# Layer 0's projection of a two-layer diffusion transformer: a fixed TensorE order, modulation in column tiles, x in half rows

## The chip, the core and the metric

The kernel runs on one core of a Trainium2 chip. Its engines work beside each other, each through its own list of instructions in order: TensorE (PE in the rows, with its weight loads as PEld), VectorE (DVE), ScalarE (ACT), GpSimd (POOL) and SyncE (SP), which here starts nearly all DMA transfers. The metric is the device time of one launch in microseconds (us), median of several runs. Lower is better.

## The reference, cut to what matters

The program computes two layers over 1024 latent tokens and 256 context tokens, 1024 features each, in float32. The change lies in the first step of layer 0: the modulation vectors, the modulated input h, and its product with the input weights.

```python
for l in range(DEPTH):
    m_lat = [m[:, None, :] for m in jnp.split(jax.nn.silu(c) @ ada_w[l] + ada_b[l], 6, axis=-1)]
    m_ctx = jnp.split(jax.nn.silu(c_ctx) @ ada_w[l] + ada_b[l], 6, axis=-1)
    h_lat = modulate(x_lat, m_lat[0], m_lat[1])      # x * (1 + scale) + shift
    h_ctx = modulate(x_ctx, m_ctx[0], m_ctx[1])
    ...
# layer 0: even_mixer -> even_project
qa, ka, va, qb, kb, vb = jnp.split(h @ w_in, [...], axis=-1)
return (rms_norm(heads(qa, A_HEADS), q_gain), rms_norm(heads(ka, A_KV_HEADS), k_gain),
        heads(va, A_KV_HEADS), heads(qb, B_HEADS), heads(kb, B_HEADS), heads(vb, B_HEADS))
```

Two kinds of attention, an output product and a convolutional feed-forward layer follow, and then layer 1. The change leaves them as they are.

## The kernel before, in words

Tokens go in ten tiles of 128: tiles 0 to 7 are latent (H[0] holds 0 to 3, H[1] 4 to 7), 8 and 9 are context (H[2]). Every operand of a product is split into a high and a low part, so one product is three matmuls for each of the eight feature blocks k (`mm3`, lines 333 to 337): 24 matmuls.

The stage `l0_project` runs in this order. `ada_first` (line 141) makes the first two modulation vectors (shift and scale) of layer 0 for the latent and the context condition: 16 loads `wt` of 512 KB, each used by two matmuls that give 2 rows x 512 columns (line 160); the sums get their bias (line 170) and are transposed in 16 pieces (line 173). Then x and the context are loaded in 10 tiles of 512 KB (lines 445 and 447), each feature block of each group is transposed (line 452), scaled and shifted by ScalarE (`sg`, line 456), and split into `hh` (line 462) and `hl` (line 464, by turns on VectorE and GpSimd). Then come five blocks of weights: columns 512 (k and v of attention A, 256 wide), 0 (its q), 1792 (v of attention B) by `proj_tok`, 768 and 1280 (q and k of attention B) by `proj_feat`. Each is loaded by `load_in` through the pool `raw`, which has two buffers of 512 KB, and split by `split` into the pool `ring` (12 buffers; the high part by ScalarE, line 99, the low part here by GpSimd, line 100). Results are normalized, rotated, transposed (`put_T`, line 412) and stored.

Beside the products runs `ada_items`: it makes four more modulation vectors of layer 0 and two of layer 1, in 12 blocks of 512 columns for two conditions. Each block loads four `araw` tiles of 512 KB and accumulates 16 times on VectorE (lines 201 and 205); then each of the two sums is split (lines 255 and 256) and added up over the partitions by two matmuls (lines 259 and 260). `bg(n)` takes n steps of it after a tile.

What sets the order: a tile scheduler places the instructions of each engine by simulated time and priority, TensorE's too in this stage. Only inside `with self.manual_pe():` does TensorE follow the order in which the program was written; before the change this holds for the attention and later stages, not for `l0_project`. A tile waits until the buffer it takes is free, and SyncE's transfers wait in one line behind each other.

```python
self.raw = ctx.enter_context(self.pool("raw", bufs=2))   # line 72
for k0 in range(0, KT, g):                               # load_in, line 110
    r = self.t(self.raw, [128, g, n], "raw")
    nc.sync.dma_start(r, wv[:, k0 : k0 + g, c0 : c0 + n])
```

## Time and profile before

| | |
|---|---|
| median of 3 runs | 3019.02 us (3016.95 to 3020.67) |
| the profiled execution | 3018.82 us, its span 3017.0 us |
| busy share of the span | PE 94%, DVE 70%, ACT 45%, POOL 23% |
| chain that ended last | PE 76%, DVE 8%, DMA 5%, ACT 4%, POOL 3% |
| `l0_project` | from 0 to about 388 us; attention follows |

The span goes from the first to the last instruction of the profiled execution; 1.8 us of its time lie around it. A busy share is a mean over stages with different limits, so what the change is worth is read in the stage that it touches, the first 388 us. There the view by stretches of time says how full each engine is, the timeline says what TensorE waited for, and the groups by line give durations.

### The profile page before, as it was taken

The numbers are of one execution on the slowest core, as the hardware profiler recorded it, in microseconds if no ns is written. First come the engines' busy times: TensorE is split into PE (matmuls) and PEld (weight loads), VectorE is DVE, ScalarE is ACT, GpSimd is POOL, SyncE is SP. The second block draws the span as 40 slices with busy tenths as digits, with TensorE's granted clock in tenths as the row PEclk, the third lists the DMA queues.
The fourth block names the chain that finished last, engine by engine and source line by source line (L and its number), as shares of the span: only waits on it lengthen the run. The fifth ranks groups of instructions, "written<-read, shape, count | busy, mean of one in ns | idle before, by whom it ended". The sixth has DMA issues, their size and how long they took to land.

```text
span 3017.0 us, 44716 instructions
## 1 busy us (share of the span) xinstructions
PE 2840.4 (94%) x16564; PEld 2286.8 (76%) x16564; DVE 2104.3 (70%) x3797; ACT 1363.5 (45%) x2589; POOL 683.8 (23%) x888
## 2 busy tenths in 40 slices
PE   6889989899999989999999998989997999999998
PEld 2767767777788977888888877766676788888886
DVE  3687756667678777888878655557776777777655
ACT  2222146567535555545453343257753555455330
POOL 3661033335361000000001013344544000000001
PEclk7899999999999999999999998999998999999999
DMA  8366741024467653333358526742144222224741
GB/s 252 89 176 212 222 137 31 26 64 148 129 160 230 207 169 104 108 116 115 108 185 308 172 77 194 219 110 64 59 149 156 88 80 82 84 84 149 269 141 75
DMA packets 348774, 418.57 MB, mean 139 GB/s; under 512 B 22938, under 2 KB 262794, under 8 KB 347018
## 3 DMA queue, kind: packets, MB, share of 16 engines
q1 hardware_dynamic: 330796, 361.31, 38.6%
q0 software_dynamic: 14864, 52.70, 4.9%
q8 instruction: 130, 2.13, 0.3%
q10 hardware_dynamic: 2896, 1.70, 0.2%
q14 instruction: 88, 0.72, 0.1%
HBM read 318.85 MB, written 96.80 MB: 138 GB/s over the span
## 4 chain that ended last, share of the span: by engine, by line
PE 76%; DVE 8%; DMA 5%; ACT 4%; POOL 3%; issue 2%; SPq 0%; ACTq 0%; POOLq 0%; DVEq 0%
PE y L1566 8%; PE q L1566 8%; PE x L1566 8%; PE d L336 5%; PE d L335 5%; PE d L337 5%; PE S L629 4%; PE v L1566 4%; PE pv L774 3%; PE T L760 3%; PE mm L337 2%; PE mm L335 2%; PE mm L336 2%; ACT P L650 2%; PE o L337 2%
## 5 line engine op out<-in xcount | busy, mean ns | idle before, releaser
L653 POOL TENSOR_SCALAR P<-P,rin 128x640 f32<-128x640 f32 (+3 forms) x288 | 250.2, 873 | 350.9 <-DVE rin L652 322.7
L1465 DVE TENSOR_TENSOR w<-raw,w 128x512 fp32r<-128x512 f32 x308 | 208.8, 691 | 166.8 <-ACT w L1463 166.7
L335 PE MATMUL d<-w,w 128*128 128x512 f32 x704 | 275.3, 391 | 0.0
L336 PE MATMUL d<-w,w 128*128 128x512 f32 x704 | 274.6, 390 | 0.0
L337 PE MATMUL d<-w,w 128*128 128x512 f32 x704 | 274.5, 390 | 0.0
L99 ACT CAST w<-raw 128x512 fp32r<-128x512 f32 x276 | 160.6, 619 | 224.8 <-PE d L337 127.8
L1613 POOL DMA_DIRECT2D g<-cv x44 | 23.5, 533 | 873.9 <-DVE cv L1612 873.9
L100 DVE TENSOR_TENSOR w<-raw,w 128x512 fp32r<-128x512 f32 x224 | 148.1, 701 | 94.0 <-ACT w L99 91.9
L629 PE MATMUL S<-k,q 64*128 64x256 f32 (+2 forms) x1824 | 192.7, 338 | 18.3 <-DVE nm L2008 8.2
L650 ACT ACTIVATE P<-P,nm 128x641 f32<-128x641 f32 (+4 forms) x208 | 161.3, 777 | 83.3 <-DVE nm L2008 47.3
L1463 ACT CAST w<-raw 128x512 fp32r<-128x512 f32 x308 | 182.5, 621 | 14.9 <-DVE raw L1470 11.1
L629 PEld LDWEIGHTS S<-k,q 64*128 64x128 f32 x1824 | 136.2, 189 | 54.0 <-issue 18.8
L640 ACT COPY PT<-T 128x512 f32<-128x512 f32 (+1 forms) x250 | 134.1, 566 | 81.2 <-PE T L760 78.9
L335 PEld LDWEIGHTS d<-w,w 128*128 128x128 f32 x704 | 132.6, 188 | 27.6
L337 PEld LDWEIGHTS d<-w,w 128*128 128x128 f32 x704 | 132.5, 188 | 27.6
L336 PEld LDWEIGHTS d<-w,w 128*128 128x128 f32 x704 | 132.6, 188 | 27.2
L1557 DVE TENSOR_TENSOR w<-raw,w 128x512 fp32r<-128x512 f32 x176 | 112.2, 685 | 50.1 <-ACT w L1556 50.0
L774 PE MATMUL pv<-PT,v 128*64 128x128 f32 x2016 | 132.8, 279 | 15.1 <-ACT PT L640 13.3
L760 PE MATMUL T<-ident,P 128*128 128x128 f32 x1008 | 136.3, 282 | 10.0 <-POOL P L653 5.9
L1701 ACT COPY ug<-q 128x512 f32<-128x512 f32 x44 | 25.8, 586 | 255.7 <-PE q L1566 255.7
L205 DVE SCALAR_TENSOR_TENSOR acc<-araw,cs,acc 128x512 f32<-128x512 f32 x168 | 132.1, 838 | 12.2 <-DMA araw<-in_ada_w_dram 11.5
L774 PEld LDWEIGHTS pv<-PT,v 128*64 128x64 f32 x2016 | 108.9, 137 | 41.0 <-ACT PT L640 22.0
(331 smaller groups left out, 7726.7 us busy)
## 6 DMA issues: line engine op xcount, KB each, us to landing
raw<-in_up_dram SPq DMA_DIRECT2D x132, 512.0 KB
raw<-g SPq DMA_DIRECT2D x88, 512.0 KB
raw<-in_down_dram SPq DMA_DIRECT2D x66, 512.0 KB
araw<-in_ada_w_dram SPq DMA_DIRECT2D x48, 512.0 KB
g<-cv POOLq DMA_DIRECT2D x44, 512.0 KB, 3.0
raw<-in_w_in_dram SPq DMA_DIRECT2D x28, 512.0 KB
araw<-in_ada_w_dram SPq DMA_DIRECT2D x40, 256.0 KB
wt<-in_ada_w_dram SPq DMA_DIRECT2D x16, 512.0 KB
```

What stands on the lines that cost most here:

```text
L99: nc.scalar.copy(hi, s)
L335: nc.tensor.matmul(ps, lh, rh, start=first, stop=False)
L336: nc.tensor.matmul(ps, lh, rl, start=False, stop=False)
L337: nc.tensor.matmul(ps, ll, rh, start=False, stop=last)
L629: self.nc.tensor.matmul(outs[a], q[r, x, qs], k[r, y, ks], start=(i == 0), stop=(i == 2))
L650: nc.scalar.activation(P[:, :m], P[:, :m], AF.Exp, bias=negm, scale=-1.0, accum_out=den)
L653: nc.gpsimd.tensor_scalar(P[:, :n], P[:, :n], rin, 1.0, ALU.mult, ALU.mult)
L760: nc.tensor.transpose(ps[:, s * 128 : (s + 1) * 128], P[a][:, cols[i + x] : cols[i + x] + 128], self.ident,)
L774: nc.tensor.matmul(O[a * HD : (a + 1) * HD], v_of(a, vts[i + x]), pT[:, s * 128 : (s + 1) * 128], start=(i + x == 0), stop=(i + x == m - 1 ...
L1463: nc.scalar.copy(half(i, 0), src[i])
L1465: nc.vector.tensor_sub(half(i, 1), src[i], f32(half(i, 0)))
L1566: nc.tensor.matmul(ps, w[:, a, s], r[b][:, k], start=first and k + i == 0, stop=k == 3 and i == 2, skip_group_check=True,)
```

## The change

`ada_first` now gives each of the four matmuls of a block k another group of 32 output rows (`tile_position`), has nine `wt` buffers, takes the bias as columns (with `c8` and `cc8` in one transposed load), and adds up the four row groups in 16 full matmuls with a selector `sel`. x and the context come in half rows: 8 buffers of 128 x 512, the first eight loads queued right behind the weights. Only group 0 (tiles 0 to 3) is transposed ahead of the products. The transposes of group 1 stand between the first four products with the k and v weights, and those of group 2 between the first four products with the q weights. The tiles 4 to 9 of both follow, then v of B, q of B and k of B. TensorE follows the written order through the whole stage. The weights' low parts move from GpSimd to VectorE, as do all `hl`; of the `hh` every second goes to ScalarE. `ada_items` keeps four parts (8 blocks instead of 12), a step that returns "hold" ends `bg`, and the two vectors of layer 1 are made by the new `ada_cols`: for each block k one load of 512 KB through the pool `raw` and four matmuls of 2 x 256 in four column groups, one step after each product of q and k of B.

```diff
-        rt = self.t(tp, [128, 128], "rt")
+        rt = self.t(tp, [128, 128], "rt", bufs=3)
...
-    def ada_first(self):
+    def ada_first(self, loads):
         nc, io = self.nc, self.io
         with ExitStack() as es:
-            tp = es.enter_context(self.pool("p0", bufs=2))
-            wp = es.enter_context(self.pool("p0w", bufs=6))
+            tp = es.enter_context(self.pool("p0"))
+            ap = es.enter_context(self.pool("p0a"))
+            wp = es.enter_context(self.pool("p0w", bufs=9))
             pp = es.enter_context(self.pool("p0s", bufs=1, space=PSUM))
-            ct = self.cols(tp, pp, [io["c8"], io["cc8"]], "ccol")
+            bias = self.row128(io["ada_b"][0, 0:2048])
+            ct = self.cols(tp, pp, [io["c8"], io["cc8"], bias], "ccol")
             self.cs = self.t(self.cst, [128, 2, 8], "cs")
             nc.scalar.activation(
-                self.cs, ct.rearrange("p (v k) -> p v k", v=2), AF.Silu
+                self.cs, ct[:, :16].rearrange("p (v k) -> p v k", v=2), AF.Silu
             )
             w = io["ada_w"][0].rearrange("(k p) n -> p k n", p=128)
             ps = [self.t(pp, [128, 512], f"a{j}") for j in range(4)]
+            for x in ps:
+                nc.vector.memset(x, 0.0)
+            ar = self.t(ap, [128, 2048], "ar")
+            sel = self.t(ap, [128, 2], "sel")
+            nc.vector.memset(sel, 0.0)
+            for g in range(4):
+                nc.vector.tensor_copy(sel[32 * g : 32 * g + 2], self.ident[:2, :2])
             for k in range(KT):
                 for h in range(2):
                     wt = self.t(wp, [128, 1024], "wt")
                     nc.sync.dma_start(wt, w[:, k, h * 1024 : (h + 1) * 1024])
                     for j in range(2):
+                        b = 2 * h + j
+                        g = (b + k) % 4
                         nc.tensor.matmul(
-                            ps[2 * h + j][:2, :], self.cs[:, :, k],
-                            wt[:, j * 512 : (j + 1) * 512],
-                            start=(k == 0), stop=(k == KT - 1),
+                            ps[b][32 * g : 32 * g + 2, :], self.cs[:, :, k],
+                            wt[:, j * 512 : (j + 1) * 512], start=k < 4, stop=k >= 4,
+                            tile_position=(0, 32 * g), skip_group_check=True,
                         )
-            br = self.t(tp, [2, 2048], "br")
-            nc.sync.dma_start(br, io["ada_b"][0, 0:2048].partition_broadcast(2))
-            ar = self.t(tp, [2, 2048], "ar")
+            loads()
             for j in range(4):
-                s = slice(j * 512, (j + 1) * 512)
-                nc.vector.tensor_add(ar[:, s], ps[j][:2, :], br[:, s])
+                d = ar[:, j * 512 : (j + 1) * 512]
+                if j % 2:
+                    nc.vector.tensor_copy(d, ps[j])
+                else:
+                    nc.scalar.copy(d, ps[j])
             pt = self.t(pp, [128, 512], "small")
             for j in range(16):
-                nc.tensor.transpose(
-                    pt[:, 2 * j : 2 * j + 2], ar[:, j * 128 : (j + 1) * 128],
-                    self.ident[:2, :2],
+                nc.tensor.matmul(
+                    pt[:, 2 * j : 2 * j + 2], ar[:, j * 128 : (j + 1) * 128], sel,
+                    start=True, stop=True, skip_group_check=True,
                 )
             m0 = self.t(self.cst, [128, 2, 8, 2], "mod0")
-            nc.vector.tensor_copy(
-                m0.rearrange("p a k v -> p (a k v)"), pt[:, :32]
+            nc.vector.tensor_add(
+                m0.rearrange("p a k v -> p (a k) v"),
+                pt[:, :32].rearrange("p (n v) -> p n v", v=2),
+                ct[:, 16:32].unsqueeze(2).to_broadcast([128, 16, 2]),
             )
             nc.vector.tensor_scalar(m0[:, 1], m0[:, 1], 1.0, None, ALU.add)
...
+    def ada_cols(self, tp, bank, l, part):
+        nc, io = self.nc, self.io
+        def load(k):
+            r = self.t(self.raw, [128, D], "raw")
+            c0 = part * D
+            nc.sync.dma_start(r, io["ada_w"][l][k * 128 : (k + 1) * 128, c0 : c0 + D])
+            return r
+        br = self.t(tp, [128, 256], "abr2")
+        for c in range(4):
+            b0 = part * D + c * 256
+            nc.sync.dma_start(
+                br[32 * c : 32 * c + 2], io["ada_b"][l, b0 : b0 + 256].partition_broadcast(2)
+            )
+        ps = bank()
+        r = load(0)
+        yield
+        for k in range(KT):
+            n = load(k + 1) if k + 1 < KT else None
+            for c in range(4):
+                nc.tensor.matmul(
+                    ps[32 * c : 32 * c + 2, :256], self.cs[:, :, k],
+                    r[:, c * 256 : (c + 1) * 256],
+                    start=(k == 0), stop=(k == KT - 1), tile_position=(0, 32 * c),
+                    skip_group_check=True,
+                )
+            r = n
+            yield
+        for c in range(4):
+            s = slice(32 * c, 32 * c + 2)
+            nc.vector.tensor_add(br[s], ps[s, :256], br[s])
+            nc.sync.dma_start(self.d["ada"][l, :, part, c * 256 : (c + 1) * 256], br[s])
...
+    def prod_tok(self, pp, hT, t, ws, n):
+        hi, lo, o = hT(t)
+        ps = self.t(pp, [128, 512], "mm")
+        for k in range(KT):
+            self.mm3(
+                ps[:, :n], hi[:, k, o : o + 128], lo[:, k, o : o + 128],
+                ws[k][0][:, :n], ws[k][1][:, :n], k == 0, k == KT - 1,
+            )
+        return ps
...
+        ex = ExitStack()
+        xp = ex.enter_context(self.pool("xp", bufs=8, side="right"))
         xs = io["x"].rearrange("(r s c) d -> s r c d", r=16, s=8, c=8)
...
+        x = {}
+        w = io["w_in0"]
+        def load_x(i, h):
+            for j in range((4, 4, 2)[i]):
+                x[i, j, h] = r = self.t(xp, [128, 512], "x")
+                c = slice(h * 512, (h + 1) * 512)
+                if i == 2:
+                    nc.sync.dma_start(r, io["ctx"][j * 128 : (j + 1) * 128, c])
+                else:
+                    nc.sync.dma_start(r, xs[4 * i + j][:, :, c])
+        def first_loads():
+            load_x(0, 0)
+            load_x(0, 1)
+        with self.manual_pe():
+            self.ada_first(first_loads)
...
-        self.conv = [self.conv_cols(l, st, pa) for l in range(2)]
+        m0 = self.mod0
+        def group(i, k):
+            n, v = (4, 4, 2)[i], 1 if i == 2 else 0
+            ps = self.t(pt, [128, 4, 128], "tr")
+            c = slice(k % 4 * 128, k % 4 * 128 + 128)
+            for j in range(n):
+                nc.tensor.transpose(ps[:, j], x[i, j, k // 4][:, c], self.ident)
+            sg = self.t(xp, [128, 4, 128], "sg", bufs=3)
+            nc.scalar.activation(
+                sg[:, :n], ps[:, :n], AF.Identity,
+                bias=m0[:, 0, k, v : v + 1], scale=m0[:, 1, k, v : v + 1],
+            )
+            hi = H[i][0][:, k].rearrange("p (j t) -> p j t", t=128)
+            lo = H[i][1][:, k].rearrange("p (j t) -> p j t", t=128)
+            if k % 2:
+                nc.scalar.copy(hi, sg[:, :n])
+            else:
+                nc.vector.tensor_copy(hi, sg[:, :n])
+            nc.vector.tensor_sub(lo, sg[:, :n], f32(hi))
+        with self.manual_pe():
+            for k in range(KT):
+                group(0, k)
+        wk = self.load_in(w, 512, 256)
...
+        late = []
+        def tok(t, ws, n, ev):
+            ps = self.prod_tok(pp, hT, t, ws, n)
+            late.append(ev(t, ps))
+            if len(late) > 3:
+                (late.pop(0) or int)()
+        with self.manual_pe():
+            load_x(1, 0)
+            load_x(1, 1)
+            wq = self.load_in(w, 0, 512)
+            for t in range(4):
+                tok(t, wk, 256, ev_kva)
+                group(1, 2 * t)
+                group(1, 2 * t + 1)
+            load_x(2, 0)
+            load_x(2, 1)
+            for t in range(4):
+                tok(t, wq, 512, ev_qa)
+                group(2, 2 * t)
+                group(2, 2 * t + 1)
+            ex.close()
+            adap = es.enter_context(self.pool("adap", side="right"))
+            ada = [
+                self.ada_items(
+                    adap, lambda: self.t(banks[0], [128, 512], "small"),
+                    [(0, part, (0, 1)) for part in (2, 3, 4, 5)], W=512, nraw=2, nacc=1,
+                )
+            ]
+            conv = self.conv = []
+            for t in range(4, NT):
+                tok(t, wk, 256, ev_kva)
+                if t in (5, 7):
+                    conv.append(self.conv_cols(len(conv), st, pa))
+                if t > 7:
+                    bg(2)
+            wv = self.load_in(w, 1792, 512)
+            for t in range(4, NT):
+                tok(t, wq, 512, ev_qa)
+                bg(3)
+            wb = None
+            for t in range(NT):
+                tok(t, wv, 512, ev_vb)
+                bg(3)
+            wb = self.load_in(w, 768, 512)
+            for f in late:
+                (f or int)()
...
+            pc = e3.enter_context(self.pool("pac", bufs=1, space=PSUM))
+            colp = e3.enter_context(self.pool("colp"))
+            side = (
+                x for part in range(2)
+                for x in self.ada_cols(colp, lambda: self.t(pc, [128, 512], "cols"), 1, part)
+            )
...
-                    bg(4)
+                    bg(3)
+                    next(side, None)
...
-            self.proj_feat(pp, chunks, w, 768, ev_feat(d["qB"], HD ** -0.5), pool)
-            self.proj_feat(pp, chunks, w, 1280, ev_feat(d["kB"], None), pool)
-            for _ in ada:
-                pass
+            with self.manual_pe():
+                self.proj_feat(pp, chunks, wb, ev_feat(d["qB"], HD ** -0.5))
+                wb = self.load_in(w, 1280, 512)
+                self.proj_feat(pp, chunks, wb, ev_feat(d["kB"], None))
+                for g in (side, ada[0]):
+                    for _ in g:
+                        pass
```

Three places in the instructions' order. Names are the tiles' (tr: transposes; mm: a product's result; small: a sum; cols: the sums of `ada_cols`; w, hh, hl: split weights and inputs; raw: unsplit weights). The first is TensorE at the start of the products, before the change:

```order
L173 MATMUL small_201<-ident_58,ar_196 128x2 x16
L452 MATMUL tr_238<-ident_58,x_230 128x128
...
L452 MATMUL tr_443<-ident_58,x_390 128x128
L452 MATMUL tr_443<-ident_58,x_392 128x128
L335 MATMUL mm_529<-w_515,hh_32_102 128x256
```

and after it:

```order
L512 MATMUL tr_339<-ident_58,x_228 128x128
L385 MATMUL mm_430<-w_351,hh_32_102 128x256
...
L387 MATMUL mm_430<-w_362,hl_33_103 128x256
L512 MATMUL tr_472<-ident_58,x_382 128x128
...
L512 MATMUL tr_481<-ident_58,x_388 128x128
L385 MATMUL mm_490<-w_351,hh_32_102 128x256
```

Before, 80 transposes stand ahead of the first product; now 32 do, and 48 stand between products. The second place is TensorE where the q weights of B give way to its k weights, after the change (mm_2673 is the last product with the former, mm_2753 the first with the latter):

```order
L387 MATMUL mm_2616<-hh_34_104,w_2109 128x512
L309 MATMUL small_2646<-ahl_2597,ones_65 128x512
L310 MATMUL small_2646<-ahl_2597,ones_65 128x512
L289 MATMUL cols_2613<-raw_2614,cs_133 2x256 x4
L385 MATMUL mm_2673<-hh_36_106,w_2082 128x256
...
L387 MATMUL mm_2673<-hh_36_106,w_2109 128x256
L289 MATMUL cols_2613<-raw_2667,cs_133 2x256 x4
L385 MATMUL mm_2753<-hh_32_102,w_2723 128x512
...
L387 MATMUL mm_2753<-hh_32_102,w_2750 128x512
L289 MATMUL cols_2613<-raw_2715,cs_133 2x256 x4
```

Before, L335 of the first product with the k weights followed L337 of the last one with the q weights. Now a column step stands between them, and its raw_2667 and the next step's raw_2715 are the two buffers of the pool from which the k weights come too. The third place is SyncE's line of transfers there, after the change:

```order
L274 DMA raw_2667<-in_ada_w_dram 128x1024
...
L274 DMA raw_2715<-in_ada_w_dram 128x1024
L112 DMA raw_2721<-in_w_in_dram 128x2x512
...
L112 DMA raw_2729<-in_w_in_dram 128x2x512
...
L112 DMA raw_2737<-in_w_in_dram 128x2x512
...
L112 DMA raw_2745<-in_w_in_dram 128x2x512
```

The four loads of the k weights (raw_2721 to raw_2745) stand behind two loads of the column steps; raw_2721 waits for TensorE, the other three for VectorE. Before, the four stood at the beginning of q of B, among its first stores.

## Rows read from the trace of the kernel before

**Rows 1.** Stretches of the stage: length, then for each engine busy us and number of instructions, granted clock of TensorE (1.00 is 2.4 GHz, 0.50 is 1.2 GHz), busy share of the DMA engines, GB/s.

```profile
0.00:84.74 84.74, 53.05 (x161) 20.96 (x162) 34.93 (x48) 22.54 (x36) 33.72 (x33) 0.75 0.73 225
84.74:388.10 303.36, 279.13 (x1399) 231.66 (x1399) 221.49 (x359) 63.84 (x134) 106.61 (x108) 0.97 0.59 181
180.00:220.00 40.00, 29.59 (x120) 22.66 (x119) 31.81 (x44) 11.52 (x21) 30.45 (x20) 0.87 0.60 177
220.00:260.00 40.00, 39.85 (x174) 32.25 (x173) 28.39 (x43) 7.34 (x13) 0.85 (x1) 1.00 0.60 192
```

**Rows 2.** The timeline of TensorE at the start: begin, length, line, operation, tiles; in brackets the idle time before and what ended it. A matmul in full float32 (L160) has two records, each with its weight load (PEld). The last row is the 24th record of the first product.

```profile
5.58 30.46 PE L160 MATMUL a<-wt,cs 128*2 128x512 f32 x64 [2.63 <-DMA wt<-in_ada_w_dram]
...
11.42 0.09 PEld L160 LDWEIGHTS a<-wt,cs 128*2 128x2 f32 x1 [0.63 <-issue]
11.85 0.09 PEld L160 LDWEIGHTS a<-wt,cs 128*2 128x2 f32 x1 [0.34 <-issue]
...
35.97 1.25 PE L173 MATMUL small<-ident,ar 2*128 2x2 f32 x16
...
82.40 0.69 PE L452 MATMUL tr<-ident,x 128*128 128x128 f32 x2 [0.60 <-ACT sg L456]
84.74 0.58 PE L335 MATMUL mm<-w,hh 128*128 128x256 f32 x1 [1.66 <-ACT sg L456]
...
89.82 0.29 PE L337 MATMUL mm<-w,hl 128*128 128x256 f32 x1
```

**Rows 3.** The timeline of SyncE's transfers at the start.

```profile
1.52 3.05 SPq L158 DMA_DIRECT2D wt<-in_ada_w_dram  x6
...
26.15 12.85 SPq L112 DMA_DIRECT2D raw<-in_w_in_dram  x4
...
39.57 4.14 SPq L447 DMA_DIRECT2D x<-in_x_dram  x6
```

**Rows 4.** Stretches again, for the last two columns: x is moved in the first, context and `raw` in the second, `wt` alone in the third.

```profile
48.00:54.00 6.00, 2.65 (x9) 1.51 (x9) 0.00 (x0) 0.33 (x1) 0.00 (x0) 0.50 1.04 248
...
66.00:72.00 6.00, 4.84 (x19) 3.64 (x19) 4.50 (x5) 3.11 (x5) 5.50 (x5) 0.50 1.04 391
4.00:12.00 8.00, 6.42 (x9) 1.05 (x10) 0.00 (x0) 0.00 (x0) 0.00 (x0) 1.00 1.01 395
```

**Rows 5.** Groups of instructions by line and form, 0 to 85 us: line, engine, operation, tiles, shapes, count, then busy us, mean ns of one, and the idle time before them with what ended it.

```profile
L452 PE MATMUL tr<-ident,x 128*128 128x128 f32 x80 | 21.2, 421 | 24.7 <-DVE acc L205 9.7 <-ACT sg L456 8.0 <-DMA x<-in_x_dram 6.9
...
L456 ACT ACTIVATE sg<-tr,mod 128x512 f32<-128x512 f32 x16 | 11.6, 774 | 20.6 <-PE tr L452 15.4 <-POOL hl L464 4.4 <-DVE hl L464 0.7
L464 POOL TENSOR_TENSOR hl<-sg,hh 128x512 fp32r<-128x512 f32 x8 | 11.2, 1395 | 15.1 <-DVE hh L462 15.1
...
L462 DVE CAST hh<-sg 128x512 fp32r<-128x512 f32 x16 | 9.6, 619 | 10.0 <-ACT sg L456 10.0
L99 ACT CAST w<-raw 128x512 fp32r<-128x512 f32 x11 | 6.4, 614 | 35.6 <-DMA raw<-in_w_in_dram 35.6
...
L170 DVE TENSOR_TENSOR ar<-a,br 2x512 f32<-2x512 f32 x4 | 2.7, 679 | 30.9 <-PE a L160 30.9
```

**Rows 6.** The same view for 220 to 260 us, where GpSimd is idle: one accumulation, and one subtraction that makes a low part.

```profile
L205 DVE SCALAR_TENSOR_TENSOR acc<-araw,cs,acc 128x512 f32<-128x512 f32 x31 | 21.6, 745 | 7.0 <-DMA araw<-in_ada_w_dram 6.9
...
L256 DVE TENSOR_TENSOR ahl<-acc,ahl 128x512 fp32r<-128x512 f32 x4 | 2.8, 693 | 0.5 <-ACT ahl L255 0.3
```

**Rows 7.** The timeline of TensorE: first matmuls of three products in a row with the k weights of B, the first 256 columns wide, the second 512.

```profile
371.34 0.28 PE L335 MATMUL mm<-hh,w 128*128 128x256 f32 x1
...
374.07 0.39 PE L335 MATMUL mm<-hh,w 128*128 128x512 f32 x1
...
379.66 0.39 PE L335 MATMUL mm<-hh,w 128*128 128x512 f32 x1
```

**Rows 8.** The timeline of TensorE in the attention: scores (64 of the array's rows at a time), values (two groups of 64 output rows by turns, two records each) and transposes.

```profile
438.98 1.66 PE L629 MATMUL S<-k,q 64*128 64x512 f32 x12
440.56 2.84 PE L774 MATMUL pv<-PT,v 128*64 128x128 f32 x48
443.34 1.53 PE L760 MATMUL T<-ident,P 128*128 128x128 f32 x12
444.80 0.98 PE L629 MATMUL S<-k,q 64*128 64x256 f32 x12
```

**Rows 9.** The timeline of SyncE and ScalarE where two loads of weights of 512 KB are started and their splitting begins.

```profile
266.81 0.42 SPq L112 DMA_DIRECT2D raw<-in_w_in_dram  x1
270.37 0.46 SPq L112 DMA_DIRECT2D raw<-in_w_in_dram  x1
271.91 1.14 ACT L99 CAST w<-raw 128x512 fp32r<-128x512 f32 x2 [7.27 <-DMA raw<-in_w_in_dram]
275.71 1.14 ACT L99 CAST w<-raw 128x512 fp32r<-128x512 f32 x2 [1.65 <-DMA raw<-in_w_in_dram]
```

**Rows 10.** What TensorE waited for in 84.74 to 388.10 us: us in total, times, longest.

```profile
PE tr L412 <- POOL q L539: 12.4, 4, 7.1
PE small L259 <- ACT ahl L255: 6.6, 4, 2.8
```

**Rows 11.** The timeline of TensorE where the attention begins.

```profile
389.26 1.69 PE L629 MATMUL S<-k,q 64*128 64x256 f32 x24 [0.92 <-PE small L129]
...
393.87 0.31 PE L129 MATMUL small<-ident,rt 48*128 48x48 f32 x1 [2.93 <-DMA rt<-ada]
```

More of the change, by code (lines that the diff above doesn't have):

```diff
@@ L556, in ev_vb @@
             self.put_v(st, ps, 8, d["vB"][t * 128 : (t + 1) * 128])
-            bg(2)
-        w = io["w_in0"]
-        order = list(range(NT))
-        pool = nc.gpsimd
-        self.proj_tok(pp, hT, order, w, 512, 256, ev_kva, pool)
-        self.proj_tok(pp, hT, order, w, 0, 512, ev_qa, pool)
-        self.proj_tok(pp, hT, order, w, 1792, 512, ev_vb, pool)
+        late = []
[44 more added lines that the diff above has]
+                (f or int)()
         e1.close()
```

62 lines of the change are left out of this document (4 added, 58 removed).

## The prediction

> **What bounds the kernel now.** I read the stretches of time first. In the first 84.74 us no product runs; TensorE is busy for 53 us of it, much of that at the lower clock (mean 0.75 of 2.4 GHz) [rows 1]. From there to 388.10 us the five blocks of products run, and TensorE is busy for 279.1 of 303.4 us; 220 to 260 us is full, 180 to 220 us lacks 10.4 us [rows 1]. So the stage has two different limits: a start that is a line of steps, each waiting for the one before, and then TensorE itself.
>
> The timeline shows the start: the matmuls of the weights take TensorE from 5.58 to 36.04 us, the first transposes come late, and the first product begins at 84.74 and ends with its 24th record at 90.1 us [rows 2]. SyncE's line shows why x is late: the weights of the products were started at 26.15 us and x only at 39.57 us, behind waits for their split [rows 3]. Then 80 transposes take 21.2 us of TensorE and 24.7 us of idle time stands before them, divided between x, ScalarE and VectorE [rows 5]. In the product part the longest waits are for GpSimd's scaling of q, 12.4 us, and for the sums, 6.6 us [rows 10].
>
> **The change part by part.** I work out when the first product ends, then what TensorE has to do after it.
>
> *Weights in column groups.* A record costs 0.43 us at the full clock (11.42 to 11.85) [rows 2]; a block k has four matmuls of two records, 3.4 us in line. The values of the attention show two groups by turns: 48 records of 128 columns in 2.78 us, 0.058 us each, where a quarter of 0.43 is 0.107 [rows 2, 8], so two groups run 1.85 times as fast. With four I expect 0.9 to 1.85 us per k. A block's load is 1.05 MB, 2.65 us at 395 GB/s [rows 4], so now the transfers set the pace: first arrival at about 5.9 us (one more small load ahead), 15 more at 1.33 us: 25.8 us, the last matmuls end at 26.7. Bound: no overlap, 36.4 us.
>
> *Modulation and x.* A copy (0.68, the form of L170) [rows 5], then 16 full matmuls; each has two records where the 16 transposes took 1.25 us [rows 2]: 2.5 us, or 5 at the lower clock. With two small steps the factors stand at about 31. The eight half loads (2.1 MB) lie right behind the weights: at x's own 248 GB/s [rows 4] 8.5 us, so the first half is there at 30.0, the second at 34.3, 1 MB of product weights at 391 GB/s [rows 4] at 37.0. Bounds for the half rows: 391 GB/s (3 us earlier) and half of 248 (8.5 us later); I take 248, the row of the same data. By the Trainium skill, "DMA: Bandwidth & Descriptors", section Measured, transfers below 1 MB lose rate, 138 GB/s at 64 KB against 341 at 1 MB. Here transfers of 512 KB ran at 395 [rows 4], so I leave it; at 138 GB/s the two halves would cost an estimated 6.7 us and the sum would be 2998.
>
> *Group 0.* ScalarE has 8 `sg` (0.77), 4 `hh` and 4 casts (0.62 each) [rows 5] from about 31.9: 11.2 us. VectorE has 12 subtractions at 0.69 [rows 6] and 4 casts at 0.62: 10.8 us, beside it. With the wait for three `sg` buffers, and 0.8 us of matmuls behind the last split weight, the first product ends at 44.3 instead of 90.1 us: 45.8 us are gained to this mark.
>
> *After the mark.* TensorE's work, with 2.73 us for a product of 256 columns and 5.59 for one of 512 [rows 7] and 0.122 for a transpose (443.34 to 444.80) [rows 8]: 9 products with the k,v weights 24.6; 20 of q and v 111.8; q and k of B 111.3; 48 transposes now between them 5.9; 50 of results 6.1; 32 matmuls of sums at 0.233 7.5 (48 before, 11.2); 16 column steps; six small transposes 1.8. A column step has 8 records of 256 columns, 1.72 us in line, 0.43 with perfect overlap, 0.93 by the factor for two groups; I take 0.6, in all 9.6. Sum 278.6. Before, the same list without the moved transposes and the column steps gives 266.8 of 298.0 us, so waits and slow clock took 31.
>
> The Trainium skill, "TensorEngine Tiling (Array Packing)", section Tiling Modes, says that changing the tiling mode drains the array, and the column steps change it 32 times. The attention goes from 64-row scores to 64-column values to full transposes with each begin before the modelled end of the one before [rows 8], so I count nothing. An estimate from the drain of some 128 cycles in "TensorE: Matmul & The Clock Gate", section "Step-by-step: what each phase is for", would be 1.7 us, and the sum 2993.
>
> *What becomes late.* The column steps take their tiles from `raw`, which has two buffers. At the change from q to k of B one is held by raw_2715 until a step that stands behind the first k product, and that product needs all four loads of k weights. They must pass one after another through the other buffer, which comes free only when raw_2667 has been used, behind the last q product. A load takes 5.1 to 5.3 us from its start to its cast [rows 9], its two casts and two subtractions 2.0 (0.62 + 2 x 0.69): 4 x 7.1 + 0.7 for the last matmuls = 29.1 us for a product of 5.6, a wait of 23.5. raw_2667 itself is started about 2.5 us after the product before last, behind a store and a sum's way through VectorE, and lands 5.1 us later, against 3.8 us of TensorE work: another 3.8. Together 27; behind the waiting matmul stands the whole rest of the list. Bounds: 10 (load 1.7, from 512 KB at 395 GB/s and 0.4 of issue, nothing ahead) and 35 (8.5 per load with the q loads of the attention between, and accumulations ahead on VectorE). The four loads stood early before, so nothing there was of this kind.
>
> Other waits: groups 1 and 2 let ScalarE and VectorE set the pace for the first four products (15.5 and 17 us against 12.8 of TensorE), but only their weights' split holds TensorE up, 3 us; the small transposes of the convolution wait in line, 2; sums 3 (7 before); column loads 3. The 12.4 us for q [rows 10] go, since GpSimd loses the subtractions (1.4 us each, as long as `hl` [rows 5]) that stood ahead of it. VectorE takes them, 36 at 0.69 = 25 us, and loses 64 accumulations at 0.745 [rows 6] = 48; its total falls. All waits: 38 us.
>
> *Sum.* 44.3 + 278.6 + 38 = 360.9 against 388.1: 27.2 less. The attention also finds its second set of factors without the 2.9 us wait [rows 11], most of which lay beside ScalarE's work: 1 us. 3018.8 - 28.2 = 2990.6; the profiled execution is 0.2 us under the median, so **2991 us**. Clock: the transposes ran at 0.50 and the first product became fast only as it ended; the same is in my sum up to 44.3. If TensorE stays at half clock through group 1 too, it costs about 5 us.
>
> **Rivals.** (a) *The two buffers don't bind*, because a buffer comes free earlier than I read from the order: 24 us less, 2967. For it speaks that the stage before had no such wait; against it the waits written in the order. (b) *Column groups don't overlap* when there are four: the weights end 9.7 us later, the steps cost 17.9 more, 3018.6, no change. Against it speaks the 1.85 of two groups. (c) *Slower: VectorE holds SyncE, and SyncE holds TensorE.* In q and k of B each column load stands behind stores of a product's result, and those wait for VectorE behind accumulations. If VectorE trails by one pair of conditions (4 x 0.745 = 3.0 us), a load starts 4.5 us after a product (1.5 for its evacuation) and lands at 9.6, against 6.2 us to its use: 3.4 us per 512 product and 6.3 per 256, over 14 steps 10 x 3.4 + 4 x 6.3 = 59, less the 3 counted: 3047. It decides from about 2 us of trail at every step, where the 28 us are gone. For it speaks VectorE's 73% in this part [rows 1]; against it that the order starts several of these loads ahead of the stores. (d) *x in half rows is slow*: 8.5 us at the start and as much for group 1 at worst, 3003 to 3008.
>
> **How the numbers follow.** Forecast 0.66, a 0.12, b 0.06, c 0.06, d 0.10. The forecast's own range is 2977 to 3005: boundary 10 to 35 us, half rows, clock. The range takes in half of (a) and all of (d): 2971 to 3010. Faster by over 0.2% (6 us, about what a measurement of this kernel can tell) are the forecast, (a) and (d) but for their tails: 0.86; within it 0.07, mostly (b); slower 0.07.
>
> **What would show it.** The end of the first product near 44 us (right from 41 to 50); `wt` matmuls ending near 27 with the DMA engines full; no GpSimd wait for q; one gap of some 25 us in short pieces near 272 to 305 us at L385 with the k weights, released by ScalarE or VectorE behind `raw` loads, the clock falling in it; column steps of 0.5 to 0.9 us; the attention's first scores near 361. Wrong: no such gap, a first product after 55 us, or waits of over 3 us at most column steps.

## The result and the profile after

The changed kernel takes **2994.62 us** (median of 4 runs, 2988.70 to 2997.19) against 3019.85 us for the kernel before beside it (4 runs): a ratio of 0.9915, 95% interval 0.9898 to 0.9933, so 25 us less. The forecast was 2991, its range 2971 to 3010. The profiled execution took 2995.48 us with a span of 2993.7.

The stretches after, in the columns of [rows 1]:

```profile
50.00:110.00 60.00, 55.92 (x371) 51.12 (x370) 43.31 (x109) 27.15 (x64) 35.71 (x51) 0.97 0.51 155
110.00:220.00 110.00, 110.00 (x501) 88.59 (x499) 87.69 (x139) 28.66 (x56) 37.16 (x27) 1.00 0.63 194
220.00:278.00 58.00, 54.81 (x317) 41.84 (x314) 35.76 (x60) 7.29 (x14) 0.00 (x0) 0.97 0.71 228
278.00:312.00 34.00, 13.78 (x44) 7.63 (x43) 12.79 (x21) 6.04 (x11) 0.00 (x0) 0.55 0.81 237
312.00:365.00 53.00, 53.00 (x290) 41.85 (x291) 9.14 (x17) 5.65 (x11) 1.07 (x4) 1.00 0.48 153
```

From 50 to 278 us TensorE is nearly full. The one hole is 278 to 312, with 13.8 busy of 34 us at a granted clock of 0.55. TensorE's timeline at the start, for [rows 2], and its first scores, for [rows 11]:

```profile
24.35 1.03 PE L171 MATMUL a<-wt,cs 128*2 128x512 f32 x4 [0.25 <-DMA wt<-in_ada_w_dram]
26.83 1.03 PE L171 MATMUL a<-wt,cs 128*2 128x512 f32 x4 [1.45 <-DMA wt<-in_ada_w_dram]
27.79 6.13 PE L185 MATMUL small<-sel,ar 128*128 128x2 f32 x32
33.77 6.41 PE L512 MATMUL tr<-ident,x 128*128 128x128 f32 x32
41.22 0.39 PE L385 MATMUL mm<-w,hh 128*128 128x256 f32 x1 [1.03 <-ACT w L99]
43.64 0.58 PE L386 MATMUL mm<-w,hh 128*128 128x256 f32 x1 [2.04 <-DVE w L100]
...
49.39 0.28 PE L387 MATMUL mm<-w,hl 128*128 128x256 f32 x1
...
368.47 1.70 PE L730 MATMUL S<-k,q 64*128 64x256 f32 x24 [0.40 <-DVE m1ab L331]
```

The matmuls of the modulation now wait for their loads (a quarter of a microsecond before each pair). The first product ends at 49.67 us (90.11 before), the first scores come at 368.47 (389.26 before). So 40.4 us are gained by the first mark, and only 20.8 are left at the second. From the scores to the end it is 2627.0 us, before 2629.6.

TensorE's waits from 50 to 365 us, for [rows 10], and its timeline at the change from q to k of B:

```profile
PE mm L385 <- ACT w L99: 18.0, 4, 8.7
PE cols L289 <- DMA raw<-in_ada_w_dram: 5.4, 3, 2.2
PE small L129 <- DVE cc L131: 4.1, 2, 2.5
```

```profile
280.53 0.62 PE L289 MATMUL cols<-raw,cs 128*2 128x256 f32 x8 [2.21 <-DMA raw<-in_ada_w_dram]
289.88 0.80 PE L385 MATMUL mm<-hh,w 128*128 128x512 f32 x1 [8.74 <-ACT w L99]
295.74 0.80 PE L385 MATMUL mm<-hh,w 128*128 128x512 f32 x1 [2.93 <-ACT w L99]
301.51 0.80 PE L385 MATMUL mm<-hh,w 128*128 128x512 f32 x1 [2.85 <-ACT w L99]
307.93 0.80 PE L385 MATMUL mm<-hh,w 128*128 128x512 f32 x1 [3.50 <-ACT w L99]
```

The waits for GpSimd and for the sums are gone. Four waits stand before the four loads of the k weights, and SyncE's line says why:

```profile
281.26 0.44 SPq L112 DMA_DIRECT2D raw<-in_w_in_dram  x1
...
291.27 0.39 SPq L112 DMA_DIRECT2D raw<-in_w_in_dram  x1
...
297.04 0.38 SPq L112 DMA_DIRECT2D raw<-in_w_in_dram  x1
...
302.81 0.37 SPq L112 DMA_DIRECT2D raw<-in_w_in_dram  x1
...
309.24 0.35 SPq L274 DMA_DIRECT2D raw<-in_ada_w_dram  x1
```

One load at a time, 5.8 us apart once they run (291.27, 297.04, 302.81), through one of two buffers; the other holds a tile of a column step until after the product. SyncE's waits from 278 to 312 us show the second to fourth load waiting for VectorE's part of the splits, which sets the one buffer free:

```profile
SPq L112 <- DVE w L100: 6.5, 3, 2.6
```

The first of the four waits, 8.74 us, has a second part. ScalarE's cast of these weights came 8.0 us after the load was started, the next one 3.8 us after its load. In ScalarE's list it stood behind a cast of a sum, which waited for VectorE's accumulations:

```profile
288.69 0.62 ACT L305 CAST ahl<-acc 128x512 fp32r<-128x512 f32 x1 [9.96 <-DVE acc L219]
289.22 1.13 ACT L99 CAST w<-raw 128x512 fp32r<-128x512 f32 x2
295.07 1.14 ACT L99 CAST w<-raw 128x512 fp32r<-128x512 f32 x2 [4.72 <-DMA raw<-in_w_in_dram]
```

How much of the 4.2 us between the two is this cast, and how much the transfers started just before the load, is not shown.

### The profile page after: what moved, and what is told of

The parts are those of the page before. It is cut to its first block, busy times and chain, and to the rows that moved or that the text cites. A ratio compares the mean times of both kernels' runs of the same rounds, so it can differ in the third digit from the quotient of the medians.

```text
span 2993.7 us, 44874 instructions
## 1 busy us (share of the span) xinstructions
PE 2836.2 (95%) x16692; PEld 2291.7 (77%) x16692; DVE 2046.6 (68%) x3768; ACT 1366.0 (46%) x2595; POOL 625.0 (21%) x840
## 4 chain that ended last, share of the span: by engine, by line
PE 81%; DVE 7%; DMA 5%; ACT 4%; issue 2%; POOL 1%; SPq 0%; ACTq 0%; POOLq 0%; DVEq 0%
PE y L1667 8%; PE q L1667 8%; PE x L1667 8%; PE d L385 5%; PE d L386 5%; PE d L387 5%; PE S L730 5%; PE v L1667 4%; PE mm L385 4%; PE mm L386 3%; PE mm L387 3%; PE pv L875 3%; PE T L861 3%; PE pv L835 2%; PE T L826 2%; PE o L387 2%
## 5 line engine op out<-in xcount | busy, mean ns | idle before, releaser
L754 POOL TENSOR_SCALAR P<-P,rin 128x640 f32<-128x640 f32 (+3 forms) x288 | 250.8, 875 | 350.4 <-DVE rin L753 315.9
L1566 DVE TENSOR_TENSOR w<-raw,w 128x512 fp32r<-128x512 f32 x308 | 208.8, 691 | 164.8 <-ACT w L1564 164.7
L385 PE MATMUL d<-w,w 128*128 128x512 f32 x704 | 275.2, 391 | 0.0
L99 ACT CAST w<-raw 128x512 fp32r<-128x512 f32 x276 | 160.9, 620 | 186.6 <-PE d L387 127.4
L100 DVE TENSOR_TENSOR w<-raw,w 128x512 fp32r<-128x512 f32 x260 | 170.4, 696 | 107.7 <-ACT w L99 105.4
L751 ACT ACTIVATE P<-P,nm 128x641 f32<-128x641 f32 (+4 forms) x208 | 161.4, 777 | 82.9 <-DVE nm L2109 46.7
L1564 ACT CAST w<-raw 128x512 fp32r<-128x512 f32 x308 | 182.6, 621 | 15.2 <-DVE raw L1571 11.4
L385 PEld LDWEIGHTS d<-w,w 128*128 128x128 f32 x704 | 132.6, 188 | 27.5
L1658 DVE TENSOR_TENSOR w<-raw,w 128x512 fp32r<-128x512 f32 x176 | 112.3, 686 | 52.0 <-ACT w L1657 51.9
L1657 ACT CAST w<-raw 128x512 fp32r<-128x512 f32 x176 | 98.8, 618 | 87.2 <-PE d L387 70.1
```

What stands on the lines that cost most here:

```text
L100: (lo_eng or nc.vector).tensor_sub(lo, s, f32(hi))
L385: nc.tensor.matmul(ps, lh, rh, start=first, stop=False)
L751: nc.scalar.activation(P[:, :m], P[:, :m], AF.Exp, bias=negm, scale=-1.0, accum_out=den)
L754: nc.gpsimd.tensor_scalar(P[:, :n], P[:, :n], rin, 1.0, ALU.mult, ALU.mult)
L1564: nc.scalar.copy(half(i, 0), src[i])
L1566: nc.vector.tensor_sub(half(i, 1), src[i], f32(half(i, 0)))
```

## Experiments

Twelve kernels, each an edit of the changed one. Three marks of each profiled execution (end of the first product; begin of the last evacuation of q of B and, in the next column, how much later the first of k begins; first scores) divide the difference; run 10 has no first mark, since its order turns four products into one another. The ratio is to the kernel before on the same chip. The runs come in four sets (the changed kernel; 1 to 4; 5 to 8; 9 to 12), in which the kernel before took 3016.22 to 3019.85 us, so medians of different sets can differ by 3.6 us for that alone. The ratios allow for it; 0.001 of a ratio is 3.0 us. Each row of marks is one execution.

| kernel | median us | ratio, 95% | first product | last q | to first k | scores |
|---|---|---|---|---|---|---|
| before | 3019.85 | 1 | 90.1 | 327.6 | 10.7 | 389.3 |
| changed | 2994.62 | 0.9915 (0.9898-0.9933) | 49.7 | 278.4 | 32.6 | 368.5 |
| 1 one group per block | 2993.06 | 0.9910 (0.9893-0.9926) | 46.3 | 272.7 | 35.0 | 365.2 |
| 2 steps pause | 2972.25 | 0.9846 (0.9832-0.9861) | 49.3 | 275.7 | 13.3 | 347.3 |
| 3 and half the loads early | 2974.10 | 0.9852 (0.9838-0.9867) | 47.3 | 277.0 | 12.5 | 350.4 |
| 4 low parts on GpSimd | 3017.96 | 1.0001 (0.9992-1.0011) | 54.0 | 301.4 | 36.9 | 395.8 |
| 5 one group for all | 2999.80 | 0.9942 (0.9927-0.9957) | 52.6 | 279.1 | 35.2 | 372.1 |
| 6 transposes first | 3000.94 | 0.9947 (0.9932-0.9962) | 65.6 | 283.7 | 32.9 | 373.7 |
| 7 sums, not column steps | 2989.01 | 0.9903 (0.9886-0.9920) | 46.7 | 277.2 | 6.1 | 353.0 |
| 8 one group per tile | 2990.66 | 0.9912 (0.9895-0.9928) | 43.3 | 273.7 | 33.3 | 364.3 |
| 9 full rows of x | 3003.56 | 0.9954 (0.9938-0.9969) | 51.5 | 279.4 | 33.7 | 371.5 |
| 10 scheduler's order | 2976.79 | 0.9868 (0.9853-0.9883) | - | 270.6 | 27.8 | 348.9 |
| 11 = 2 and 8 | 2968.42 | 0.9840 (0.9826-0.9854) | 44.0 | 274.2 | 14.0 | 346.7 |
| 12 = 11, all loads ahead | 2972.85 | 0.9858 (0.9840-0.9875) | 45.5 | 274.0 | 8.9 | 343.8 |

**The change from q to k.** Run 2:

```
-                    next(side, None)
+                    if f < 3 or dst is not d["qB"]:
+                        next(side, None)
```

> The column steps of the modulation pause during the last quarter of q of B (three products), so that no column load holds one of the two raw buffers when the k weights are loaded; all 16 steps are done, in the products of k. My theory (the wait at the change from q to k comes from four loads that pass through one free buffer): the first two k loads start about one product earlier and overlap, the waits of TensorE at the k weights (18.0 us, plus 2.2 us for the last column load) fall to 2 to 8 us, and less of the first k product runs at the lower clock: 2976 us (2970 to 2983). Rival (the loads are late because SyncE reaches them late, behind the stores of q, and the transfers of the attention's first tiles stand between): the waits stay above 14 us and the run takes 2990 to 2995.

Measured 2972.25, 22 us less (21 by the ratios), inside my numbers. The first two loads start together at 261.45 instead of 281.26 and 291.27, and of the waits from 50 to 365 us these concern the products (the second line, and others like the third, stand in the changed kernel too):

```profile
PE mm L387 <- DVE w L100: 4.4, 1, 4.4
PE small L129 <- DVE cc L131: 4.1, 2, 2.4
...
PE cols L289 <- DMA raw<-in_ada_w_dram: 2.6, 2, 1.4
...
PE mm L385 <- ACT w L99: 1.0, 1, 1.0
```

No transfer, product or step was removed, only the tile that held the buffer, and the way from the last q to the first k evacuation fell from 32.6 to 13.3 us. This shows the cause of most of the hole. Run 3 splits half the weights before the last three q products:

```
-                wb = self.load_in(w, 1280, 512)
+                wc = self.load_in(w, 1280, 512, ks=(0, 4))
+                self.proj_feat(pp, chunks, wb, ev, range(3, 4))
+                wb = wc + self.load_in(w, 1280, 512, ks=(4, 8))
```

> As the run with the pause, and the first half of the k weights is loaded and split before the last three products of q of B instead of behind them (four of the twelve split-weight buffers are free there). My theory: the first half stands ready when the last q product ends, the second half needs its buffers from that product and is 2 to 6 us late: a further 3 to 6 us less than the run with the pause, about 2971 us (2966 to 2978). Rival (ScalarE and VectorE stand in the way, since the casts now go ahead of the evacuation of the last q products, or the second half sets the end all the same): the same time as the run with the pause, within 2 us, or more.

The rival held: 2974.10. The second half still sets the end, with one wait of 5.3 us at L385; ahead of that split ScalarE's cast of a sum waited 7.91 us for accumulations.

**The column steps themselves.** Run 7 returns both parts to VectorE (`side = iter(())`, two more parts in `ada_items`, `bg(4)`):

> The last two parts of the modulation (those of the second layer) are accumulated on VectorE as before the change, instead of in column steps on TensorE; the rest as in the changed kernel. My theory (the column steps are a loss on this path: 10.3 us of TensorE, 5.4 us of waits for their loads, and some 18 us at the change from q to k because they hold the raw buffers): 16 more matmuls of sums cost 6.5 us and some waits for VectorE 5 us, the rest goes: about 2977 us (2968 to 2986). Rival (VectorE, which gets 64 accumulations of 0.745 us = 48 us back, then becomes late in q and k of B, and TensorE waits for sums and evacuations): 2992 us or more.

Missed by 12 us: 2989.01. The hole went as I said (6.1 us to the first k evacuation), but TensorE then waited for sums in the k products, and in the attention for its late factors:

```profile
PE small L309 <- ACT ahl L305: 14.0, 7, 4.7
...
PE small L129 <- DMA rt<-ada: 2.9, 1, 2.9
PE small L129 <- issue: 2.2, 1, 2.2
PE small L310 <- DVE ahl L306: 2.0, 5, 0.7
```

The scores come 15.5 us earlier than in the changed kernel, but from there to the end this execution takes 2638.1 us instead of 2627.0; the 5.1 us for the factors are part of that. So column steps are no loss. With a free buffer (run 2) they are 17 us better than the sums; without one they are 4 to 6 us worse, and there the intervals of the two ratios overlap.

**The low parts.** Run 4 gives them back to GpSimd (`nc.gpsimd` in all five `load_in`, and in every second group of x):

> The low parts of all weights of this stage, and of every second tile group of x, are made on GpSimd again, as before the change; the order of TensorE stays. My theory (the 12.4 us wait for GpSimd's scaling of q went because these subtractions of 1.4 us each left GpSimd): waits for GpSimd come back at the transposes of results or at the weights, 8 to 16 us in all; first product 3 to 6 us later, since two more 1.4 us subtractions per pair stand in its chain: 3004 us (2999 to 3012). Rival (the fixed order with results transposed three products later gives GpSimd enough time): no wait for GpSimd above 2 us in the products, and only the start changes, 2994 to 3000.

2.5 times the price I had put on it: 3017.96, the whole gain of the change. No wait for the scaling of q came back. The wait now stands at the weights, and the hole grew by 4.3 us:

```profile
PE mm L385 <- ACT w L99: 20.4, 4, 8.5
PE mm L386 <- POOL w L100: 11.3, 5, 3.8
```

```profile
L100 POOL TENSOR_TENSOR w<-raw,w 128x512 fp32r<-128x512 f32 x36 | 50.9, 1440 | 138.4 <-ACT w L99 138.3
```

1.44 us for one low part, where VectorE in the changed kernel took 0.69 at the change from q to k and 0.74 in the mean of its 36. Weights and x were not tried apart.

**Column groups at the start.** Run 1 puts the four matmuls of a block into one group (`g = k % 4`):

> The four matmuls of one block k of the modulation go into the same column group (group k mod 4) instead of four different ones; sums, transfers and everything after are as in the changed kernel. My theory (the groups work beside each other, which leaves the transfers as the pace of this step): in line a block costs 3.4 us, 64 records of 0.43 us are 27.5 us and some waits, so the last of these matmuls ends at 35 to 37 us instead of 27.9, the first product 7 to 9 us later than 49.5, and the run takes about 3003 us (2999 to 3006). Rival (the gain at this step came from the loads alone, nine buffers and x behind them): no change, 2993 to 2997, and the last matmul stays below 30 us.

My theory missed, and the rival's number came for another reason. The 64 records in one line took 21.6 us and ended with the loads:

```profile
5.89 21.62 PE L171 MATMUL a<-wt,cs 128*2 128x512 f32 x64 [2.41 <-DMA wt<-in_ada_w_dram]
27.45 3.73 PE L185 MATMUL small<-sel,ar 128*128 128x2 f32 x32
```

At 0.43 us a record that is 50 places for 64 records: at each change of group two stood beside each other. Run 5 leaves no change of group (`g = 0`, sums from the first block to the last):

> All 32 matmuls of the modulation go into one and the same column group (group 0), so that no two of them can stand beside each other; sums, transfers and the rest as in the changed kernel. Theory after the run with one group per block (there 64 records of 0.43 us began at some 50 times, two at once at each change of group, and that was just enough to keep up with the transfers): now 64 x 0.43 = 27.5 us, from 5.9 to 33.4 us or a little more, 5.5 us behind the changed kernel's 27.9; the clock stays at full, so the 16 sum matmuls take 3.7 us and not 6.1, and x has landed by then; the first product ends 2 to 5 us later than 49.5, the run 2993 to 3000 us. Rival (the transfers alone set the pace, the groups bring nothing at all): the last matmul ends at 28 us again.

```profile
5.97 29.05 PE L171 MATMUL a<-wt,cs 128*2 128x512 f32 x64 [2.44 <-DMA wt<-in_ada_w_dram]
34.95 3.73 PE L185 MATMUL small<-sel,ar 128*128 128x2 f32 x32
```

29.05 us, ended at 35.0, 7 us late; 3 of these reach the first product and 5 the end (2999.80; 8 by the ratios). Overlap of groups is real and needed, but little of it is enough to keep up with the loads.

**The modulation's sum.** Run 8 keeps a tile in its own group, so that nothing has to be added over groups:

```
-                        g = (b + k) % 4
+                        g = b
...
-                nc.tensor.matmul(
-                    pt[:, 2 * j : 2 * j + 2], ar[:, j * 128 : (j + 1) * 128], sel,
+                nc.tensor.transpose(
+                    pt[:, 2 * j : 2 * j + 2], ar[:, j * 128 : (j + 1) * 128],
+                    self.ident[:2, :2],
```

> Each of the four output tiles of the modulation keeps one column group of its own over all eight blocks, so that its two rows are the finished sum; they are copied to rows 0 and 1 and turned by 16 small transposes of two rows as before the change, instead of 16 matmuls over 128 rows that add four groups. Four groups still work beside each other. My theory (the 16 matmuls, 6.1 us where I had counted 2.5, are what made the factors late): the transposes take 1.3 to 2 us, the factors stand 4 to 5 us earlier, near 30 us; of that x, whose second half lands near 33.5, lets 3 to 4.5 us through; first product ends at 45 to 46.5 and the run takes 2990.5 us (2988 to 2993). Rival (the start does not pass on what is saved there, because x or the split of the weights holds it): first product within 1.5 us of 49.5, no change.

2990.66. Three transposes of x begin at 27.91 and the other 29 at 29.39 instead of 33.77, now behind x itself (`[0.47 <-DMA x<-in_x_dram]` in that row), and the first product ends 6.4 us earlier, of which the scores keep 4.2. Three profiles have this start (runs 8, 11, 12: 43.3 to 45.5 us to the first product's end) and four the changed kernel's (that one and runs 2, 3, 7: 46.7 to 49.7), so the gain at the first mark is shown. In the total it is not: 4 us by the medians, 1 by the ratios, whose intervals overlap.

**Order and rows.** Run 6 writes the transposes of groups 1 and 2 ahead of the first product:

> The fixed order with the transposes of groups 1 and 2 ahead of the first product instead of between the first eight; nothing else. My theory (the interleaving hides the evacuations of these groups behind products): ScalarE needs about 11 us for group 1 and 6 for group 2, of which TensorE's own 6 us of transposes lie beside it, so the first product comes some 12 to 18 us later, at half clock through all of that, and the run takes 3008 us (3002 to 3014). Rival (what was gained at the start is due to the early x and the short modulation; the products after it wait for other things, such as VectorE, which catches up): no more than 5 us, below 3000.

The first product came 16 us later, as expected, but the total was only 6 us up, 3000.94: just below my range, at the edge of the rival's. By the ratios it is 10 us, inside my range, so the total doesn't decide between the two. By the last q product 5.3 us are left. The 6.2 us of transposes no longer stand between the products, and the convolution's small transposes wait 2.0 instead of 4.1 us; the rest I did not locate. Run 9 loads x in full rows:

> x and the context are loaded in full rows of 1024 numbers (512 KB a load, four buffers) instead of half rows (256 KB, eight buffers); the same bytes, and the rest as in the changed kernel. My theory (the bytes set the time of x, since halves moved at 258 to 295 GB/s, no slower than the 248 of full rows before; but the transposes of group 0 now need all of x, and group 1 finds its buffers only when a whole tile of group 0 is used up): no change to 3 us later, 2994 to 2998. Rival (smaller transfers cost rate): 3 to 7 us faster, 2988 to 2992.

Slower than either theory, 3003.56. The profiled execution, 2999.76, is the fastest of the four; it shows 3.0 us at the scores, with waits of 2.8 us for x. The rest it doesn't show. The last column has the rate of x, in the changed kernel and then in run 9:

```profile
30.00:32.00 2.00, 2.00 (x11) 2.00 (x11) 0.00 (x0) 0.00 (x0) 0.00 (x0) 0.50 1.05 285
```

```profile
30.00:32.00 2.00, 1.16 (x6) 0.76 (x6) 0.37 (x2) 0.00 (x0) 0.00 (x0) 0.50 1.06 242
```

So halving x cost no rate: the halves moved faster. The Trainium skill, "DMA: Bandwidth & Descriptors", section Measured, has transfers below 1 MB lose rate; between 512 and 256 KB these traces don't agree (its transfers were issued from GpSimd, these by SyncE). Run 10 leaves the order of all products to the scheduler (`with self.manual_pe():` taken from both blocks of products):

> The products of the stage and the transposes between them are written as in the changed kernel, but TensorE's order there is left to the scheduler, as before the change (the modulation and group 0 keep the fixed order). In its order the transposes of groups 1 and 2 stand in twos and fours among the matmuls of a product and weights of one step stand apart. My theory (the work and its sources stay the same, and a transpose waits for little): within 5 us, 2990 to 3000. Rival (the fixed order is what keeps TensorE from standing in front of a tile that is not ready): waits for ScalarE and VectorE at the transposes and weights, 3003 us or more.

Neither expected this: 2976.79, 18 us **faster** without the fixed order (14 by the ratios). The scheduler puts two column steps ahead of the first k product, and TensorE waits there for their loads, 11.1 us in all; at the k weights (L385) its waits fall from 18.0 to 1.1 us:

```profile
275.36 1.03 PE L289 MATMUL cols<-raw,cs 128*2 128x256 f32 x8 [4.80 <-DMA raw<-in_ada_w_dram]
282.65 1.03 PE L289 MATMUL cols<-raw,cs 128*2 128x256 f32 x8 [6.26 <-DMA raw<-in_ada_w_dram]
```

By the marks 7.8 us of the gain lie before the last q product, 4.8 at the change and 7.0 after the first k evacuation. These 7.0 belong to the change too: of column steps only one fewer is left there (5, not 6), but the matmuls of several k products use each pair of weights as it comes. The third product, 256 columns wide, has begun before the first evacuation at 298.4:

```profile
295.66 0.28 PE L385 MATMUL mm<-hh,w 128*128 128x256 f32 x1
```

At the start its order does the same with four products, where the fixed order finishes one product and waits for the next split (2.04 us at 43.64 in the changed kernel). Which of these differences brings how much was not tried apart.

**Together.** Run 11 has the edits of runs 2 and 8:

> Two edits of earlier runs together: the column steps pause in the last quarter of q of B, and each output tile of the modulation keeps its own column group, with 16 small transposes. If they act in different places, as I hold, their gains add: -22 and -4 from 2994.6: 2968 us (2964 to 2973). Rival (what the start gives is lost at the next wait, a wait for VectorE or a load): 2971 to 2975, as with the pause alone.

2968.42, where the sum has it: the lowest median of the study, 1.6% below the kernel before and 26 us below the changed one (23 by the ratios). That the gains add is not shown, though. Against run 2 the first product ends 5.3 us earlier, but the last q evacuation comes only 1.5 and the first scores 0.6 us earlier, and the two profiled executions took 2970.59 and 2970.60 us; the ratios, 0.9840 and 0.9846, have overlapping intervals. In q of B TensorE waited for one column load longer than run 2 did for the same one (1.17 us), and the granted clock of q of B was 0.97 where run 2 had 1.00:

```profile
236.13 0.61 PE L284 MATMUL cols<-raw,cs 128*2 128x256 f32 x8 [3.44 <-DMA raw<-in_ada_w_dram]
```

So the rival, that the start's gain is lost at a later wait, is not ruled out. Run 12 also starts all four loads ahead of the last q products:

> As the run with both edits, and the four loads of the k weights are started ahead of the last two products of q of B, one after another, and split as soon as their buffers allow, instead of behind the stores of the last product. In the run with the pause alone the third load was started at 278.1 us, behind those stores, and TensorE then waited 4.4 + 1.0 us for its split. My theory: that wait falls to 1 to 3 us (its buffers of split weights come free only with the last q product), 2 to 5 us less than with both edits, about 2965 us. Rival (the split waits for ScalarE behind a cast of the sums, which waits for VectorE's accumulations, whenever the load lands): the same time within 2 us, or more, as when the first half alone was loaded early.

The change from q to k shortened by 5.1 us and the scores came 2.9 us earlier, as the theory has it; the median rose to 2972.85. Whether that is a loss stays open: the intervals of the two ratios overlap, and the profiled execution, which took 13.3 us more than run 11's after the scores, is the slowest of its four (2981.03). The scheduler's order together with these edits was not run.

## Why the prediction was right

**The boundary** was the step that mattered, and it held: 27 us foreseen. The distance from the last q to the first k evacuation is 32.6 us, against 6.1 where the loads stand ready (run 7): 26.5, of which 20.2 are waits (the five rows); the rest is the column step and work at the lower clock. Run 2 shows the cause. The parts were less exact than their sum, which is some luck: loads 5.8 us apart where I had 7.1, a wait of 2.2 us for raw_2667 where I had 3.8, but 8.6 us from the start of the first load to its first matmul, where the cast behind VectorE's accumulations, which I had only in the upper bound, took its share. Rival (a), 2967 if the buffers don't bind, is thereby a kernel one can write; run 2 came to 2972.

**The weights** ended at 27.86 (26.7 foreseen), held by loads every 1.28 us (1.33). **First product:** 49.67 against 44.3, at the edge of what I had called right. The mis-sized term is the 16 full matmuls of the modulation: I took 2.5 us, with 5 at the lower clock as a bound, and they took 6.13. They began right behind the weights, so the factors stood at 34.34 where I had about 31. The other 2 us came behind them: the granted clock had fallen to 0.50, and most of the transposes and of the first product's matmuls ran at that level.

**After the mark** I had 316.6 us, and the k products end 317.6 after it. The waits came to less than 38: boundary 26.5, columns 3.2 elsewhere (3 foreseen), the convolution's transposes 4.1 (2), sums 0 (3), first four products 0 (3), in all 33.8. The work is therefore some 5 us more than my list; I didn't find where. A column step took 0.61 to 0.62 us (0.6) at the full clock. The attention gained 2.5 (1). In sum 5.4 + 1.0 - 1.5 is 4.9 us above the forecast's 2990.6, which is the 2995.48 of the profiled execution. That 5 us more of work met 4 us less of waits is luck.

Rivals (b) to (d) are out. Run 5 prices missing overlap at the start at 5 to 8 us, and it isn't missing. Column loads were waited for three times, 2.2 us at most, so SyncE doesn't hold TensorE. Nothing waited for x in half rows.

What the sum could not see was the worth of the parts. It gave the low parts 12.4 us, by the wait that would go; undone in the new order, with every second group of x, they cost 23. And it gave TensorE's fixed order no price, where the scheduler's order is 18 us faster (14 by the ratios). Some 12 of these lie between the last q and the scores, at the same hole as run 2's 22, so the two are not separate parts.

## What to carry over

In an order written by hand, a step that holds a shared buffer blocks every later user of the pool until its place comes; list for each change of weights who holds the buffers then, and let side work pause there. A right total can be made of large parts of both signs (here the low parts gained 23 us and the held buffer lost 22), so undo the parts one at a time; what the undoings bring need not add, as runs 2 and 10 shorten the same hole. A wait that stood at one instruction returns at another when its cause returns, so the wait's own length is no price for the cause.

## What was not expected of the hardware

The same start met different clocks. The 32 records of the modulation's sum took 6.1, 5.2, 4.0 and 3.7 us in the changed kernel and in runs 2, 6 and 7, though the program is the same up to there. The stretch of 2 us from 28 us, of the changed kernel and then of run 7:

```profile
28.00:30.00 2.00, 2.00 (x15) 2.00 (x14) 0.62 (x1) 0.47 (x1) 0.00 (x0) 0.69 1.06 289
```

```profile
28.00:30.00 2.00, 2.00 (x20) 2.00 (x19) 0.00 (x0) 0.00 (x0) 0.00 (x0) 1.00 1.05 295
```

The granted clock fell from 2.4 to 1.2 GHz within the first and stayed at 2.4 through the second, after the same pairs of matmuls with gaps of a quarter of a microsecond before them and a longer one before the last pair (1.45 and 1.09 us). That gap doesn't sort the runs: it was 1.08 us in run 4 and 1.09 in run 7, and the 32 records took 5.66 and 3.73 us. The first product ends at 49.7 and 46.7 us: single profiles of one start differ by that much without a cause in the program, and of run 8's 6.4 us some may be this.

The two matmuls of one load, in two column groups, ran as four records in 1.03 us where a line of 0.43 takes 1.72; a column step, four groups of 256 columns, took 0.61 us for its eight records.
